# Moving six chunks of a modulation matrix product from TensorE to VectorE

## The chip, the cores and the metric

The kernel runs on one core of a Trainium2 chip. The metric is the device time of one execution in microseconds (us), as the median of three runs; lower is better. The engines are named as in the profile: PE is TensorE (matmul), PEld its weight loads, DVE VectorE, ACT ScalarE, POOL GpSimd, SP SyncE. Here SP issues the DMA loads of the weights.

## The reference

Two transformer blocks over 256 tokens of 1024 features, all in float32. The first has an attention and pooling mixer and a mixture of 32 experts. The second is modulated by a vector that comes from a condition `c`:

```python
def second_block(x, c, w_ada, b_ada, norm1_g, norm2_g, w_in, ...):
    mod = jax.nn.silu(c) @ w_ada[l] + b_ada[l]          # (1, 1024) @ (1024, 6144)
    sh1, sc1, g1, sh2, sc2, g2 = jnp.split(mod[:, None, :], 6, axis=-1)
    hn = (_rms(x, norm1_g[l]) * (1 + sc1) + sh1).astype(x.dtype)
    y = _mixer(hn, w_in[l], ...)
    x = x + g1 * (y.astype(x.dtype) @ w_out[l])
    hn = (_rms(x, norm2_g[l]) * (1 + sc2) + sh2).astype(x.dtype)
    gate, up = jnp.split(hn @ w_gate_up[l], 2, axis=-1)
    x = x + g2 * ((jax.nn.silu(gate) * up) @ w_down[l])
    return x
```

The change concerns the first line, `mod`. It doesn't depend on `x`, so it can be computed whenever the weights are there.

## The kernel before

The program has these stages, in the times of the trace: the first block's mixer and the router (here called the head, 0 to about 108 us); its experts, for which 2 MB loads of weights stream in (to about 1029 us); the second block's mixer (to about 1199 us): the modulated input is transposed into columns, projected part by part (`fv`, `mo`, `fq`, `fk`, `mqk`, ... in the order of the table `PROJ`), and goes through three kinds of heads; then its feed-forward part, to the end.

Weights are loaded into a ring of slots. SP issues the loads in one order, each as soon as slots are free (`pump`); the program gives slots back with `release`. A weight that is used as a split in two float32r halves goes through `split`: ACT writes the high half (L311, or with a gain L318), DVE the low half (L312, or L319).

`mod` is made from 24 chunks of 1 MB of `w_ada`, called `("ada", i)`, 128 rows by 2048 columns (the last eight 2 x 128 rows by 1024). `GRPS` cuts them in runs: chunks 0 to 7 (needed for the mixer's input, computed in the head), 8 to 15 (the gate `g1`, computed in the mixer), 16 to 19 and 20 to 23. A run ends in 512 x 4 sums that ACT copies out (L881). `MODE` has a letter for each chunk:

- `p`: PE multiplies. Four matmuls (L873), one for each quarter of 512 columns, with 32 copies of a column of `cs` (silu of `c`) as the weights, sit on four column groups of the array and add into one PSUM tile. Below, these four are called a group.
- `d`: DVE multiplies the chunk's four quarters by `cs` in place. The first of a run does only that (L853); each later one adds the chunk before (L855), whose slots are then released. The last sum goes through PE as one more group, with ones instead of `cs`.

The first `p` of a run stands behind its `d`s, so the sum by ones comes in the group after. `ada_step` and `ada_to` are called at set places of the program (`ASTEP`, `QSTEP` and `STEPS` in the head, `ADAT` in the mixer). A scheduler then places each engine's instructions; those under `keep_in_program_order` keep their order among themselves. In the head, chunk 3 to 7 come between the attention pairs; beside them stand the attention's scaling of its result `ya` (L679), its transposition (L687), the pooled half's `bt` (L817) and the splits `wl` (L319) of the first block's output projection `w_op`. In the mixer, `modulate` computes for each pair of 128 features `ht` (DVE), the high half of `cols` (ACT) and the low half (DVE); `gates` is a chain of small DVE operations from `z` to `gl`; `heads` computes for `fq` and `fk` squares on ACT (L1439), their sums (L1440), a reciprocal root in short steps (L354 to L363) and the scaling (L1443) on DVE, and PE then transposes the result (L1451).

Of the kernel before, what the change touches and what calls it, by code (L numbers as in the profile page):

```python
# [156 lines left out]
W_R = ((0, 2), (2, 2), (4, 4))  # L157
WARM = (14, 24)
BD_AT = (9, 6)
MODE = "ddddpppp" "pppppppp" "ddpp" "pppp"  # L160
GRPS = (0, 8, 16, 20, 24)
STEPS = (3, 2, 0, 0)
ASTEP = 2
# [11 lines left out]
class Net:  # L175
# [655 lines left out]
    def ada_setup(self):  # L831
        nc, c = self.nc, self.const
        self.cs = c.tile([P, KD], F32, name="cs")
        v = self.vcol("c_2", 0, KD)
        nc.scalar.activation(self.cs, v, AF.Exp, bias=0.0, scale=-1.0)
        nc.vector.tensor_scalar(self.cs, self.cs, 1.0, None, op0=OP.add)
        nc.vector.reciprocal(self.cs, self.cs)
        nc.vector.tensor_tensor(self.cs, self.cs, v, op=OP.mult)
        self.mod = c.tile([P, 48], F32, name="mod")
        self.adan, self.aacc = 0, None  # L840
        self.mr = c.tile([P, 512], F32, name="mr")

    def ada_step(self, n):
        nc = self.nc
        for i in range(self.adan, self.adan + n):
            o, m, k, nk = ADA[i]
            first, last = i in GRPS, i + 1 in GRPS
            w = self.chunk(("ada", i)).rearrange("p a (b c) -> p (a b) c", c=512)
            if MODE[i] == "d":
                for j in range(4):  # L850
                    c = self.cs[:, k + j * nk // 4:k + j * nk // 4 + 1]
                    if first:
                        ins = nc.vector.tensor_scalar(w[:, j], w[:, j], c, None, op0=OP.mult)  # L853
                    else:
                        ins = nc.vector.scalar_tensor_tensor(w[:, j], w[:, j], c, self.aacc[1][:, j], op0=OP.mult, op1=OP.add)  # L855
                    self.tc.keep_in_program_order(ins)
                if not first:
                    self.release(self.aacc[0])
                self.aacc = ("ada", i), w
                if not last:  # L860
                    continue
            pieces = []
            if MODE[i] == "p":
                pieces.append((("ada", i), w, [self.cs[:, k + j * nk // 4:k + j * nk // 4 + 1] for j in range(4)]))
            if self.aacc and (last or MODE[i] == "p"):
                pieces.append((*self.aacc, [self.ones[:, 0:1]] * 4))
                self.aacc = None
            if first or MODE[i - 1] == "d":
                self.adap = self.tr()
                self.adas = True  # L870
            for x, (key, w, cs) in enumerate(pieces):
                for j in range(4):
                    ins = nc.tensor.matmul(self.adap[32 * j:32 * j + 32, :], lhsT=cs[j].to_broadcast([P, 32]), rhs=w[:, j],  # L873
                                           start=self.adas, stop=last and x == len(pieces) - 1, skip_group_check=True,
                                           tile_position=(0, 32 * j))
                    if j == 0:
                        self.tc.keep_in_program_order(ins)
                self.adas = False
                self.release(key)
            if last:  # L880
                nc.scalar.copy(self.mr, self.adap)  # L881
        self.adan += n

    def ada_to(self, n):
# [1013 lines left out]
```

## Time and profile before

| | |
|---|---|
| median of three runs | 1392.44 us (1392.4 to 1392.58) |
| profiled execution | 1393.41 us, span 1391.7 us |
| granted clock of PE, mean | 0.986 of full speed |
| PE busy | 1298.2 us, 93% of the span |
| DVE busy | 557.3 us, 40% |
| ACT busy | 313.3 us, 23% |
| weight traffic | 494.04 MB, 355 GB/s on the mean |

The span is the time between the first and the last instruction of the one profiled execution; 1.7 us lie around it. Busy shares are means over stages that have different limits; the stretches below tell them apart.

### The profile page before, as it was taken

To read this page: it belongs to the slowest core of one execution; us is meant where nothing else is said; L and a number is where in the kernel's file an instruction comes from. 1 tells how busy PE (TensorE), PEld (TensorE's weight loads), DVE (VectorE), ACT (ScalarE), POOL (GpSimd) and SP (SyncE) were. 2 spreads that over 40 slices of the span, in tenths; PEclk is the share of its full clock that TensorE was granted. 3 is DMA by queue.
4 is the path that set the end of the run, shared out by engine and by line. 5 is a ranking of instruction groups with operands and counts; after the bars stand their busy time and mean duration, and the time that the engine had idled before them with its cause. 6 is when DMAs were issued, how large, how long until landed. Compare 5 with 4: busy or idle time off the path is not lost. (4 is left out here: it accounts for less than half of the span.)

```text
span 1391.7 us, 17149 instructions
## 1 busy us (share of the span) xinstructions
PE 1298.2 (93%) x6988; PEld 705.6 (51%) x6988; DVE 557.3 (40%) x1163; ACT 313.3 (23%) x602; POOL 49.0 (4%) x161
## 2 busy tenths in 40 slices
PE   9999999999999989889879998989789999999998
PEld 8674333333333333233323333333238887799997
DVE  6753322222323222132311222222247877655555
ACT  5650000000000000000000000000045556544443
POOL 7200000000000000000000000000000000000000
PEclk9999999999999999999989999999999999999999
DMA  9689999999999999999999999999988464555520
GB/s 386 244 336 428 426 427 427 428 427 425 417 428 427 427 427 428 427 428 426 428 424 426 427 427 427 428 428 428 410 356 320 165 256 153 222 189 188 189 93 31
DMA packets 42470, 494.04 MB, mean 355 GB/s; under 512 B 4720, under 2 KB 4976, under 8 KB 8720
## 3 DMA queue, kind: packets, MB, share of 16 engines
q1 hardware_dynamic: 42240, 492.78, 85.2%
q8 instruction: 57, 0.93, 0.3%
q14 instruction: 29, 0.24, 0.0%
q10 hardware_dynamic: 144, 0.10, 0.0%
HBM read 491.81 MB, written 1.05 MB: 354 GB/s over the span
## 5 line engine op out<-in xcount | busy, mean ns | idle before, releaser
L1102 PE MATMUL acc<-ring,xg 128*64 128x512 f32 x1264 | 290.8, 608 | 12.9 <-DMA ring<-in_moe_dram 12.9
L1102 PE MATMUL acc<-extra,xg 128*64 128x512 f32 x784 | 176.8, 596 | 9.5 <-DMA extra<-in_moe_dram 9.5
L1102 PEld LDWEIGHTS acc<-ring,xg 128*64 128x64 f32 x1264 | 88.1, 139 | 191.6 <-issue 161.7
L312 DVE TENSOR_TENSOR ring<-ring,ring 128x1024 fp32r<-128x1024 f32 (+4 forms) x108 | 121.1, 1130 | 87.1 <-ACT ring L311 82.1
L1130 PE MATMUL tr<-ring,aT 128*64 128x512 f32 x640 | 144.7, 596 | 9.4 <-DMA ring<-in_moe_dram 8.6
L297 PEld LDWEIGHTS tr<-cols,ring 128*128 128x128 f32 x1056 | 128.0, 192 | 1.7 <-ACT cols L1349 0.8
L297 PE MATMUL tr<-cols,ring 128*128 128x256 f32 x1056 | 128.9, 283 | 0.0
L311 ACT CAST ring<-ring 128x1024 fp32r<-128x1024 f32 (+4 forms) x108 | 104.1, 974 | 103.9 <-PE tr L297 65.3
L1241 DVE TENSOR_SCALAR gc<-acc 128x512 f32<-128x512 f32 x32 | 22.1, 692 | 259.1 <-PE acc L1102 243.4
L1161 DVE SCALAR_TENSOR_TENSOR x<-tr,G,x 128x512 f32<-128x512 f32 x128 | 87.8, 744 | 74.6 <-PE tr L1157 74.6
L1102 PEld LDWEIGHTS acc<-extra,xg 128*64 128x64 f32 x784 | 53.5, 137 | 116.8 <-issue 97.5
L1137 DVE TENSOR_TENSOR uc<-tr,gc 128x512 fp32r<-128x512 f32 x32 | 22.1, 692 | 213.3 <-ACT gc L1136 213.3
L1242 ACT ACTIVATE sg<-gc 128x512 f32<-128x512 f32 x32 | 20.2, 632 | 342.8 <-DVE gc L1241 342.8
L1130 PEld LDWEIGHTS tr<-ring,aT 128*64 128x64 f32 x640 | 44.9, 137 | 92.0 <-issue 76.7
L1130 PE MATMUL tr<-extra,aT 128*64 128x512 f32 x384 | 86.6, 596 | 0.1
L1136 ACT CAST gc<-tr 128x512 fp32r<-128x512 f32 x32 | 18.8, 586 | 242.4 <-PE tr L1130 242.4
L297 PE MATMUL acc<-ring,cols 128*128 128x384 f32 (+3 forms) x384 | 69.3, 330 | 1.1 <-ACT cols L1349 0.5
L1119 ACT ACTIVATE aT<-tr 128x512 f32<-128x512 f32 x32 | 19.1, 598 | 214.0 <-PE tr L1117 214.0
L297 PEld LDWEIGHTS acc<-ring,cols 128*128 128x128 f32 x384 | 61.3, 188 | 9.0 <-issue 5.7
L1057 DVE SCALAR_TENSOR_TENSOR xg<-tr,vt,rg 128x256 f32<-128x256 f32 x60 | 26.2, 479 | 92.7 <-PE acc L1102 88.4
L297 PE MATMUL acc<-ring,q 128*128 128x512 f32 x176 | 56.7, 394 | 0.0
L1130 PEld LDWEIGHTS tr<-extra,aT 128*64 128x64 f32 x384 | 26.9, 137 | 48.4 <-issue 46.9
(429 smaller groups left out, 1314.6 us busy)
## 6 DMA issues: line engine op xcount, KB each, us to landing
ring<-in_moe_dram SPq DMA_DIRECT2D x117, 2048.0 KB, 37.2
extra<-in_moe_dram SPq DMA_DIRECT2D x73, 2048.0 KB, 38.5
ring<-in_rest_dram SPq DMA_DIRECT2D x69, 1024.0 KB, 6.9
ring<-in_rest_dram SPq DMA_DIRECT2D x11, 768.0 KB, 5.3
ring<-in_moe_dram SPq DMA_DIRECT2D x4, 1024.0 KB, 13.0
ring<-in_rest_dram SPq DMA_DIRECT2D x2, 780.0 KB, 12.0
ring<-in_rest_dram SPq DMA_DIRECT2D x3, 512.0 KB, 9.9
ring<-in_rest_dram SPq DMA_DIRECT2D x2, 528.0 KB, 7.1
```

The lines of the kernel that those rows point to most:

```text
L297: self.nc.tensor.matmul(out, lhsT=l, rhs=r, start=start, stop=stop, skip_group_check=True)
L311: i = nc.scalar.copy(hi, w)
L312: j = nc.vector.tensor_tensor(lo, w, hi, op=OP.subtract)
L1057: nc.vector.scalar_tensor_tensor(x[:, j, :], p[:, j * 256:(j + 1) * 256], self.vcol("g_ffn_norm", k + j), rg, op0=OP.mult, op1=OP.mult)
L1102: nc.tensor.matmul(d[64 * s:64 * s + 64, :], lhsT=xg[g, k - k % 2][:, k % 2, i * CAP:(i + 1) * CAP], rhs=w[:, o + s * 512:o + (s + 1) * 51 ...
L1119: nc.scalar.activation(aT.rearrange("p a b -> p (a b)"), p, AF.Copy, scale=0.5)
L1130: nc.tensor.matmul(pd[64 * s:64 * s + 64, :], lhsT=aT[:, k % 4, (k // 4) * 64:(k // 4) * 64 + 64], rhs=w[:, k % n, s * 512:(s + 1) * 512], ...
L1136: i = nc.scalar.copy(yh, pd)
L1137: j = nc.vector.tensor_tensor(yl, pd, yh, op=OP.subtract)
L1161: ins = nc.vector.scalar_tensor_tensor(d, p, self.G[:, tt, e:e + 1], d, op0=OP.mult, op1=OP.add)
L1241: nc.vector.tensor_scalar(gc, pg, 7.0, None, op0=OP.min)
L1242: nc.scalar.activation(sg, gc, AF.Tanh, scale=0.851)
```

## The change

Chunks 4 and 5 of the first run and 10 to 13 of the second change from `p` to `d`. As the `d`s of the second run no longer stand at its start, the code asks for the running sum (`self.aacc`) rather than for the run's start, and keeps the PSUM tile (`self.adap`) over the `d`s in between.

```diff
-MODE = "ddddpppp" "pppppppp" "ddpp" "pppp"
+MODE = "ddddddpp" "ppddddpp" "ddpp" "pppp"
...
-        self.adan, self.aacc = 0, None
+        self.adan, self.aacc, self.adap = 0, None, None
...
-                    if first:
+                    if not self.aacc:
                         ins = nc.vector.tensor_scalar(w[:, j], w[:, j], c, None, op0=OP.mult)
                     else:
                         ins = nc.vector.scalar_tensor_tensor(w[:, j], w[:, j], c, self.aacc[1][:, j], op0=OP.mult, op1=OP.add)
                     self.tc.keep_in_program_order(ins)
-                if not first:
+                if self.aacc:
                     self.release(self.aacc[0])
...
-            if first or MODE[i - 1] == "d":
+            if self.adap is None:
                 self.adap = self.tr()
                 self.adas = True
...
             if last:
                 nc.scalar.copy(self.mr, self.adap)
+                self.adap = None
```

In numbers: in the head, L873 has three groups instead of five, and DVE eight more L855. In the mixer (chunks 8 to 15), five groups instead of eight (8, 9, 14, the sum by ones, 15), and on DVE four more L853 and twelve more L855. Lines behind L858 have numbers higher by one in the changed kernel.

Where the scheduler puts them. First DVE in the head, around the scaling `ya` of one attention pair. Before:

```order
L532 RECIPROCAL sm_680<-sm_680 128x4
L855 SCALAR_TENSOR_TENSOR ring_61<-ring_61,cs,ring_65 128x512 x4
L679 TENSOR_TENSOR ya_756<-tr_709,sm_680 128x256
L532 RECIPROCAL sm_760<-sm_760 128x4
L319 SCALAR_TENSOR_TENSOR wl_902<-ring_64,vt,wh_901 128x512 x2
L319 SCALAR_TENSOR_TENSOR wl_920<-ring_64,vt,wh_919 128x512 x2
L689 TENSOR_TENSOR ring_66<-tr_779,ring_66 128x256
```

and now:

```order
L532 RECIPROCAL sm_680<-sm_680 128x4
L855 SCALAR_TENSOR_TENSOR ring_61<-ring_61,cs,ring_65 128x512 x4
L855 SCALAR_TENSOR_TENSOR ring_61<-ring_61,cs 128x512 x4
L855 SCALAR_TENSOR_TENSOR ring_62<-ring_62,cs,ring_61 128x512 x4
L679 TENSOR_TENSOR ya_751<-tr_709,sm_680 128x256
L532 RECIPROCAL sm_755<-sm_755 128x4
L817 TENSOR_SCALAR bt_799<-acc_798,psc_296,pbc_298 128x256
L524 ISA s_845,m_846<-acc_849,mask 128x128
L524 ISA m_846 128x1
```

The eight new L855 stand directly behind the four that were there, ahead of `ya`; the splits `wl` that followed `ya` stand further behind. On PE at that place the groups L873 (two chunks and the ones) stood before the transposition of `ya` (tr_779). Before:

```order
L297 MATMUL tr_733<-mg_300,t_74_536 128x128 x2
L297 MATMUL tr_733<-mg_300,t_74_536 128x16
L873 MATMUL tr_742<-ring_61,cs 32x512 x4
L873 MATMUL tr_742<-ring_61,ones 32x512 x4
L873 MATMUL tr_742<-ring_62,cs 32x512 x4
L687 MATMUL tr_779<-ident,ya_756 128x128 x2
L541 MATMUL tr_786<-ident,s_758 128x128 x3
L541 MATMUL tr_791<-ident,s_758 128x128 x3
L297 MATMUL acc_803<-t_118_717,ring_86 128x256
```

and now:

```order
L297 MATMUL tr_733<-mg_300,t_74_536 128x128 x2
L297 MATMUL tr_733<-mg_300,t_74_536 128x16
L297 MATMUL acc_798<-t_118_717,ring_86 128x256
L297 MATMUL acc_808<-t_118_717,ring_86 128x256
L297 MATMUL acc_849<-cols_552,cols_551 128x128
L297 MATMUL acc_849<-cols_552,cols_551 128x256
L297 MATMUL acc_857<-cols_552,cols_551 128x128
L297 MATMUL acc_857<-cols_552,cols_551 128x256
L687 MATMUL tr_774<-ident,ya_751 128x128 x2
```

The three groups are gone from here (three now stand further behind); a projection of the pooled half and scores come instead.

Second, DVE in the mixer where the input is modulated. Before:

```order
L1348 SCALAR_TENSOR_TENSOR ht_18180<-acc_18124,A_1379,rw_18169 128x256 x2
L1348 SCALAR_TENSOR_TENSOR ht_18188<-acc_18129,A_1379,rw_18169 128x256
L1350 SCALAR_TENSOR_TENSOR cols_18179<-ht_18180,mod,cols_18178 128x256 x2
L1368 TENSOR_TENSOR ring_18083<-ring_63,ring_18083 128x780
L1350 SCALAR_TENSOR_TENSOR cols_18179<-ht_18188,mod,cols_18178 128x256
L1348 SCALAR_TENSOR_TENSOR ht_18188<-acc_18129,A_1379,rw_18169 128x256
L1348 SCALAR_TENSOR_TENSOR ht_18195<-acc_18134,A_1379,rw_18169 128x256 x2
L312 TENSOR_TENSOR ring_18083<-ring_62,ring_18083 128x780
L1350 SCALAR_TENSOR_TENSOR cols_18179<-ht_18188,mod,cols_18178 128x256
```

and now, with `ring_65` the slot of chunk 10:

```order
L1349 SCALAR_TENSOR_TENSOR ht_18179<-acc_18124,A_1379,rw_18169 128x256 x2
L853 TENSOR_SCALAR ring_65<-ring_65,cs 128x512 x4
L1351 SCALAR_TENSOR_TENSOR cols_18178<-ht_18179,mod,cols_18177 128x256 x2
L1369 TENSOR_TENSOR ring_18083<-ring_63,ring_18083 128x780
L1349 SCALAR_TENSOR_TENSOR ht_18187<-acc_18129,A_1379,rw_18169 128x256 x2
L1349 SCALAR_TENSOR_TENSOR ht_18194<-acc_18134,A_1379,rw_18169 128x256
L1351 SCALAR_TENSOR_TENSOR cols_18178<-ht_18187,mod,cols_18177 128x256 x2
L1351 SCALAR_TENSOR_TENSOR cols_18178<-ht_18194,mod,cols_18177 128x256
L1349 SCALAR_TENSOR_TENSOR ht_18194<-acc_18134,A_1379,rw_18169 128x256
```

The four L853 stand between the first `ht` and the first `cols`, and the split (L312) that stood among the columns has moved behind them.

Third, where `fq` and `fk` are scaled, DVE. Before, from the first `fq` scaling on:

```order
L1443 TENSOR_TENSOR sq_18479<-acc_18399,rsh_18483 128x384
L1443 TENSOR_TENSOR sq_18479<-acc_18400,rsh_18483 128x384
L312 TENSOR_TENSOR ring_18083<-ring_62,ring_18083 128x1024 x2
L1440 TENSOR_REDUCE ms_18559<-sq_18560 128x12
L354 TENSOR_SCALAR ms_18559<-ms_18559 128x12
L355 TENSOR_SCALAR rth_18565<-ms_18559 128x12
L356 TENSOR_SCALAR rsh_18564<-rth_18565 128x12
L361 TENSOR_TENSOR rth_18565<-rsh_18564 128x12
```

and now:

```order
L361 TENSOR_TENSOR rth_18488<-rsh_18487 128x12
L362 TENSOR_TENSOR rth_18488<-rth_18488,ms_18482 128x12
L363 SCALAR_TENSOR_TENSOR rsh_18487<-rth_18488,rsh_18487 128x12
L1441 TENSOR_REDUCE ms_18563<-sq_18564 128x12
L361 TENSOR_TENSOR rth_18488<-rsh_18487 128x12
L354 TENSOR_SCALAR ms_18563<-ms_18563 128x12
L362 TENSOR_TENSOR rth_18488<-rth_18488,ms_18482 128x12
L355 TENSOR_SCALAR rth_18569<-ms_18563 128x12
L363 SCALAR_TENSOR_TENSOR rsh_18487<-rth_18488,rsh_18487 128x12
L356 TENSOR_SCALAR rsh_18568<-rth_18569 128x12
L1444 TENSOR_TENSOR sq_18483<-acc_18403,rsh_18487 128x384
L1444 TENSOR_TENSOR sq_18483<-acc_18404,rsh_18487 128x384
```

`sq_18564` are the squares of `fk`, `sq_18483` those of `fq` (before: `sq_18560` and `sq_18479`). The sum for `fk` (L1440, now L1441) stood behind the scaling of `fq` and now stands ahead of it, in the middle of `fq`'s steps. PE transposes the scaled `fq` behind the last matmuls of `fk` and ahead of `mqk` (acc_18594) in the changed kernel:

```order
L297 MATMUL acc_18504<-ring_18122,cols_18177 128x384
L297 MATMUL acc_18504<-ring_18122,cols_18178 128x384
L297 MATMUL acc_18504<-ring_18122,cols_18177 128x384
L1452 MATMUL tr_18584<-ident,sq_18483 128x128 x3
L297 MATMUL acc_18594<-cols_18177,ring_18083 128x256
L297 MATMUL acc_18594<-cols_18178,ring_18083 128x256
L1452 MATMUL tr_18589<-ident,sq_18483 128x128 x3
```

and in the one before as well:

```order
L297 MATMUL acc_18500<-ring_18122,cols_18178 128x384
L297 MATMUL acc_18500<-ring_18122,cols_18179 128x384
L297 MATMUL acc_18500<-ring_18122,cols_18178 128x384
L1451 MATMUL tr_18580<-ident,sq_18479 128x128 x3
L1451 MATMUL tr_18585<-ident,sq_18479 128x128 x3
L297 MATMUL acc_18590<-cols_18178,ring_18083 128x256
L297 MATMUL acc_18590<-cols_18179,ring_18083 128x256
```

Only the work on DVE that feeds this transposition has moved.

## Rows read from the trace of the kernel before

**Rows 1.** The page: busy time, share and instructions of each engine.

```profile
PE 1298.2 (93%) x6988; PEld 705.6 (51%) x6988; DVE 557.3 (40%) x1163; ACT 313.3 (23%) x602; POOL 49.0 (4%) x161
```

**Rows 2.** Busy time of the engines by stretches, granted clock, DMA share, GB/s.

```profile
55.00:80.00 25.00, 24.80 (x170) 18.44 (x169) 17.10 (x52) 19.07 (x58) 0.00 (x0) 1.00 0.52 194
66.00:72.00 6.00, 6.00 (x48) 4.63 (x48) 2.98 (x9) 4.63 (x13) 0.00 (x0) 1.00 0.00 0
90.00:100.00 10.00, 9.89 (x58) 7.82 (x56) 4.68 (x8) 4.61 (x12) 0.53 (x2) 1.00 1.00 408
100.00:1000.00 900.00, 827.87 (x4019) 317.18 (x4020) 241.74 (x417) 65.00 (x115) 10.09 (x30) 0.98 1.01 426
1040.00:1100.00 60.00, 59.08 (x399) 51.03 (x399) 45.86 (x132) 33.64 (x62) 0.00 (x0) 1.00 0.68 260
```

**Rows 3.** Waits of the DMA queue (SP), 50 to 100 us: total, times, longest.

```profile
SPq L248 <- DVE wl L319: 16.6, 2, 11.6
```

**Rows 4.** SP's issues around 90 us: start, duration.

```profile
90.14 0.33 SPq L248 DMA_DIRECT2D ring<-in_moe_dram  x1
```

**Rows 5.** DVE in order of time, head: start, duration, line, [idle before].

```profile
51.66 2.71 DVE L855 SCALAR_TENSOR_TENSOR ring<-ring,cs,ring 128x512 f32<-128x512 f32 x4
54.28 0.42 DVE L679 TENSOR_TENSOR ya<-tr,sm 128x256 f32<-128x256 f32 x1
...
88.70 1.41 DVE L319 SCALAR_TENSOR_TENSOR wl<-ring,vt,wh 128x512 fp32r<-128x512 f32 x2 [0.50 <-ACT wh L318]
```

**Rows 6.** PE in order of time, head.

```profile
56.07 1.06 PE L873 MATMUL tr<-ring,cs 128*32 128x512 f32 x8
...
58.78 0.44 PE L687 MATMUL tr<-ident,ya 128*128 128x128 f32 x2
...
64.02 0.73 PE L297 MATMUL acc<-wh,ring 128*128 128x512 f32 x2 [0.20 <-ACT ring L819]
```

**Rows 7.** One line's instructions (L855, L853): ns min/median/max, first and last start.

```profile
L855 DVE SCALAR_TENSOR_TENSOR ring<-ring,cs,ring x12: 722/746/937, 34.9 to 1119.4; 128x512 f32<-128x512 f32 x12
...
L853 DVE TENSOR_SCALAR ring<-ring,cs x8: 474/482/708, 33.0 to 1105.7; 128x512 f32<-128x512 f32 x8
```

**Rows 8.** The chain of waits, 1030 to 1095 us: start, duration, what.

```profile
1041.46 0.49 DVE cols L1350
...
1042.00 7.71 PE acc L297 x41
1049.71 0.99 PE tr L873 x8
```

**Rows 9.** PE in order of time, mixer.

```profile
1038.08 1.06 PE L873 MATMUL tr<-ring,cs 128*32 128x512 f32 x8
...
1057.81 1.06 PE L873 MATMUL tr<-ring,cs 128*32 128x512 f32 x8
...
1078.37 0.82 PE L1451 MATMUL tr<-ident,sq 128*128 128x128 f32 x6
1078.94 5.99 PE L297 MATMUL acc<-cols,ring 128*128 128x256 f32 x48
```

**Rows 10.** DVE in order of time, mixer.

```profile
1054.16 0.71 DVE L312 TENSOR_TENSOR ring<-ring,ring 128x528 fp32r<-128x528 f32 x1 [3.01 <-ACT ring L311]
...
1067.75 0.18 DVE L1511 SCALAR_TENSOR_TENSOR gl<-z,gq 128x20 f32<-128x20 f32 x1
...
1075.28 1.02 DVE L1443 TENSOR_TENSOR sq<-acc,rsh 128x384 f32<-128x384 f32 x2
...
1079.09 0.95 DVE L1440 TENSOR_REDUCE ms<-sq 128x12 f32<-128x768 f32 x1 [0.46 <-ACT sq L1439]
```

**Rows 11.** One more stretch, as in rows 2.

```profile
38.00:44.00 6.00, 5.55 (x23) 3.63 (x23) 5.69 (x26) 2.88 (x6) 5.41 (x30) 0.72 0.76 315
```

**Rows 12.** PE in order of time, 34 to 50 us.

```profile
38.45 1.10 PE L297 MATMUL acc<-ring,t 128*128 128x512 f32 x2 [2.12 <-issue]
```

## The prediction

> **What bounds the kernel now.** I read the page first. TensorE (PE) is busy 93% of the span, VectorE (DVE) 40% [rows 1]; that alone would say that whatever is taken from PE is time won. The stretches say more [rows 2]. From 100 to 1000 us, the expert stage, the DMA share is 1.01 at 426 GB/s: the weights set the pace there, and what PE saves before or in it counts only if the stream of weights starts earlier. When it starts is in the view of the DMA queue's waits: the queue (SP) issues in order, each load waiting for its ring slots, and some of the longest waits of the head are for DVE's split of the output projection (wl, L319) [rows 3]. From the issue at 90.14 on [rows 4] the DMA share is 1.00 [rows 2]; the last of those splits starts at 88.70 and takes 1.41 us [rows 5]. From 1040 to 1100 us PE is busy 59.1 of 60 us and DVE 45.9 [rows 2]: there PE sets the pace, except where a short chain on DVE stands in front of it. So two places matter: how late the head's last splits are, and how far PE gets in the mixer of block 2.
>
> **The price of one chunk.** On PE a chunk is a group of four overlapping matmuls; three groups fill the time from 56.07 to 58.78 [rows 6], 0.9 us each, and one that stands alone holds the chain of waits for 0.99 us [rows 8]. On DVE it is four multiply-adds (L855) of 722 to 937 ns, or four multiplies (L853) of 474 to 482 ns at the median if it is the first of a run [rows 7]. The four of L855 at 51.66 delay the next start to 54.28 [rows 5]: 2.62 us. Four of L853 come to 4 x 0.48 = 1.9 us. So DVE pays two to three times what PE saves; what counts is whether it has the time where the new work lands.
>
> **Head.** Two chunks move (4 and 5). PE issues three groups where it had five (one by ones remains): 2 x 0.93 = 1.9 us less. DVE gets 2 x 2.62 = 5.24 us, all in one place: the order shows twelve L855 in a row ahead of ya (L679). So ya starts at 51.66 + 3 x 2.62 = 59.52 instead of 54.28 and ends 0.42 later. PE, without groups at 56.07, first does projections and scores that stood behind 58.78 (some 2.4 us), is at ya's transposition (L687) at 58.5 and waits to 60.0: 1.5 us. Transposes, a projection and the value matmuls then take it to about 62.2; it next wants the w_op matmul of the pooled half, for which two bt (L817) on DVE and a cast on ScalarE must come, now behind ya and a row of scores. I walk them to 61.5, 63.0 and 64.2. PE starts that matmul at about 64.3; before it was at 64.02 [rows 6]. Nearly equal, but before two groups were still to come and now three: +0.28 + 0.95, about **+1.2 us** at the splits that free the last slots, and the expert stage passes it on whole. The two loads whose slots the moved chunks themselves free come later too, but the DMA engines moved nothing from 66 to 72 us [rows 2], so these are hidden; if that gap were not there, they would cost their 1.5 us as well. Bounds: -1.9, if only PE's saving counts; +5.2, if all of DVE's work is exposed, which its idle time of 7.9 of the 25 us from 55 to 80 [rows 2] speaks against.
>
> **Mixer, modulation.** Before, chunk 10 ran on PE at 1038.08 [rows 9] in a gap in which PE waited for the modulated columns, so taking it away saves nothing. Now its four multiplies stand on DVE between the first ht (L1349; L1348 before) and the first cols (L1351; L1350): +1.9 us in the chain of waits that releases PE at 1042.00 [rows 8]. DVE's splits fall behind the cols, so PE's projection fv, which ended at 1049.7, ends at about 1052.1 by my walk, with four matmuls of the next one (mo, 0.13 each) done: +2.5 - 0.5 = **+2.0 us**.
>
> **Mixer, mo and the gate chain.** PE saves chunks 11 and 12 here, 2 x 0.99 [rows 8]. DVE gets eight multiply-adds, 5.24 us, in front of the last split for mo; the gap there is 3.01 us [rows 10]. They can start once the second z is there, about 1053.5, and end at 1058.8; with the split (0.71) it is 1059.5. PE has mo matmuls until about 1057.5, then waits 2.1 us, and mo ends at 1060.65 where it ended at 1057.81 [rows 9]. The gate chain behind it, on DVE alone, ended at 1067.93 with gl [rows 10] and now at about 1070.3: **+2.4 us so far**, with PE's saving in it.
>
> **Mixer, the heads.** Chunk 13 stands right behind gl, 2.6 us. The order costs more. Before, DVE scaled fq (L1443) at 1075.28 [rows 10], well before PE transposed it (L1451) at 1078.37, and with that PE went straight on to the 5.99 us of mqk [rows 9]. Now DVE's second sum of squares (L1441, for fk) stands ahead of the first L1444, and it waits for the end of fk on PE. PE in turn has the transposes of fq (L1452) right behind fk and ahead of mqk: each waits for the other's next step. From the end of fk, about 1079.9 now, it takes 0.7 to the sum's start (1079.09 against 1078.37 before [rows 9, 10]), 0.95 for the sum, some 0.7 for six short steps of two interleaved chains, and 0.5 for one scaling: 2.85 us until 1082.8, against 1078.37. **+4.4 us in all for the mixer**; what follows is the same work for PE. Bounds: -3.0 (three groups of 0.99 saved, all of DVE's 9.8 us in its 14.1 us of idle time from 1040 to 1100 [rows 2]); +7 (the three waits 2.0 + 2.1 + 2.85 with no saving against them).
>
> **The clock.** After PE's idle 2.12 us up to 38.45 the granted clock was 0.72 on the mean from 38 to 44 [rows 11, 12], a mixture of its levels 2.4 and 1.2 GHz; 0.28 x 6 = 1.7 us of PE were lost, say 1.5. Shorter waits may leave it alone; which of them do, this row can't tell. The change makes waits of about 1.5, 2 (modulation), 2.1 and 2.85 us. I take one such drop: **+1.5 us**, between 0 and 4 x 1.5 = 6. The Trainium skill, "TensorE: Matmul & The Clock Gate", part 1, says that an idle PE falls back to half its clock and gets the rest only by being busy again; it speaks against any change that opens gaps on a full PE, and the trace agrees with the 0.72 behind 2.12 us. Taken for all four waits, that would make the last term 6 and not 1.5.
>
> **Slots.** A chunk on DVE keeps its ring slot until the next one has read it, and 10 to 13 hold theirs some 10 us longer, so loads behind them start later. By the waits I get fq1 landed at 1058.7 (wanted at 1060.5) and mqk1 at 1084.6 (wanted from 1085). That is hidden, barely: cost 0; if one is late, 1 to 4 us.
>
> **Sum.** 1.2 + 4.4 + 1.5 = +7.1 us on the profiled execution's 1393.4: 1400.5. The runs' median is 1.0 lower (1392.44): **1399.5 us**.
>
> **Rivals.** *PE's saving is what counts* (faster). The new work lands in DVE's idle time, and PE is shorter by 1.9 us in the head and 3.0 in the mixer. For it: rows 2. Against it: three places where the new work stands ahead of what PE wants next. It holds if DVE is through at each of them before PE gets there: 1392.4 - 4.9 = 1387.5; half of it, 1390. Chance 0.12. The Trainium skill, "Perfetto Trace Analysis", identifying the most-contended engine, would relieve the most occupied engine first, PE here by busy time, though it warns that matmul busy time is a poor measure.
>
> *It cancels.* The third group of the head hides in a wait (0 to +0.3), no clock drop, fk's wait half as long: +0 to +2.5, 1392 to 1395. Chance 0.2.
>
> *The forecast*, 1396 to 1403: chance 0.5.
>
> *Loads or clock on top*: mqk1 or fq1 late, or the clock falls in three or four places: 1403 to 1408. Chance 0.18.
>
> **Numbers.** The runs shown lie within 0.2 us; 0.2%, 2.8 us, is about what can be told from no change, so faster is below 1389.7 and slower above 1395.2: 0.1, 0.2 and 0.7. The range leaves out half of the first rival and the end of the last: 1390 to 1405.
>
> **What would show it.** ya (L679) at 59.5; PE idle 1.5 us before L687 and 2 us before the first w_op matmul; the issue that was at 90.14 at about 91.4, and all of the expert stage as much later; the first cols 1.9 us later against ht; a wait of PE for the last mo split, and one of 2 to 3 us for sq (L1444) before L1452; a granted clock under 1.00 between 1040 and 1100. I am wrong if the issue comes before 90, if PE doesn't wait for sq, or if DVE is through with the eight multiply-adds before PE wants the split.

## The result and the profile after

The changed kernel takes 1407.32 us (median of six runs, 1406.58 to 1408.58); the kernel before took 1392.51 us on the same chip. The ratio is 1.0097 (95% interval 1.0086 to 1.0109): 13.5 us slower, or 12.0 to 15.2 (14.8 by the two medians). The direction was forecast, the size was not: 1399.5 us was the number and 1405 the end of the range. The profiled execution took 1408.58 us, span 1406.9, against 1391.7.

Busy times on the page of the changed kernel, for [rows 1]:

```profile
PE 1303.6 (93%) x6948; PEld 712.1 (51%) x6948; DVE 571.3 (41%) x1187; ACT 313.0 (22%) x602; POOL 49.2 (3%) x161
```

PE has 40 records fewer, the five groups of eight, and is busy 5.4 us longer: what is left takes longer. The stretches show where (columns as in [rows 2]: busy time of PE, PEld, DVE, ACT and POOL, then granted clock, DMA share and GB/s):

```profile
35.00:46.00 11.00, 8.93 (x36) 5.34 (x35) 10.31 (x34) 5.13 (x9) 9.28 (x42) 0.84 0.69 285
55.00:65.00 10.00, 8.26 (x50) 7.54 (x49) 7.70 (x20) 8.18 (x21) 0.00 (x0) 0.83 0.41 138
66.00:72.00 6.00, 5.57 (x29) 4.46 (x30) 5.32 (x14) 3.81 (x12) 0.00 (x0) 1.00 0.12 51
1040.00:1100.00 60.00, 52.05 (x285) 44.55 (x278) 45.37 (x115) 26.28 (x41) 0.00 (x0) 0.88 0.65 250
1042.00:1055.00 13.00, 10.41 (x43) 9.50 (x44) 11.30 (x24) 5.93 (x12) 0.00 (x0) 0.74 0.57 178
1062.00:1072.00 10.00, 7.96 (x40) 7.63 (x40) 7.55 (x16) 4.60 (x8) 0.00 (x0) 0.83 1.00 413
1088.00:1100.00 12.00, 9.17 (x63) 8.85 (x62) 9.02 (x27) 4.12 (x6) 0.00 (x0) 0.86 0.82 340
```

From 1040 to 1100 us the clock was 1.00 before [rows 2] and is 0.88 now. One minus the clock, times the length, is the time at full speed that PE lost: 3.4 us from 1042 to 1055, 1.7 from 1062 to 1072, 1.7 from 1088 to 1100, 6.8 us in the mixer, and 1.7 from 55 to 65 in the head. The first stretch (35 to 46) is the fall that was there before [rows 11]. In slices of 1 us the clock is 0.50 (1.2 GHz) from 1044 to 1050 us; from 1051 to 1062 it is 1.00 (2.4 GHz). These figures are PE's work lost; how much later the kernel ends by them is worked out below.

PE's waits from 1028 to 1100 us (total, times, longest):

```profile
PE tr L1452 <- DVE sq L1444: 2.8, 1, 2.8
PE acc L297 <- DVE ring L312: 2.0, 1, 2.0
...
PE acc L297 <- ACT cols L1350: 1.5, 1, 1.5
PE acc L297 <- DVE cols L1351: 1.4, 1, 1.4
```

PE in order of time (start, duration, [idle before]), at the places of [rows 6] and [rows 9]:

```profile
60.54 0.54 PE L687 MATMUL tr<-ident,ya 128*128 128x128 f32 x2 [1.74 <-DVE sm L532]
...
64.79 0.71 PE L297 MATMUL acc<-wh,ring 128*128 128x512 f32 x2
...
1043.05 0.45 PE L297 MATMUL acc<-ring,cols 128*128 128x390 f32 x1 [1.53 <-ACT cols L1350]
1044.88 2.00 PE L297 MATMUL acc<-ring,cols 128*128 128x390 f32 x5 [1.38 <-DVE cols L1351]
1047.04 15.29 PE L297 MATMUL acc<-ring,cols 128*128 128x390 f32 x86 [0.16 <-DVE ht L1349]
1064.37 1.91 PE L297 MATMUL acc<-ring,cols 128*128 128x264 f32 x7 [2.04 <-DVE ring L312]
...
1078.00 1.05 PE L873 MATMUL tr<-ring,ones 128*32 128x512 f32 x4
...
1079.70 1.04 PE L873 MATMUL tr<-ring,ones 128*32 128x512 f32 x2
...
1081.40 1.04 PE L873 MATMUL tr<-ring,ones 128*32 128x512 f32 x2
...
1091.80 0.90 PE L1452 MATMUL tr<-ident,sq 128*128 128x128 f32 x3 [2.83 <-DVE sq L1444]
```

Three of the waits that were forecast are there at nearly their size: 1.74 us before L687 (1.5 forecast), 2.04 for the mo split (2.1), 2.83 for sq (2.85). The modulation's wait (2 forecast) is there as two, 1.53 and 1.38 us, where the kernel before has 0.54, 0.19 and 0.34. The first of those three:

```profile
1039.69 0.45 PE L297 MATMUL acc<-ring,cols 128*128 128x390 f32 x1 [0.54 <-ACT cols L1349]
```

One is missing: PE was to idle 2 us before the first w_op matmul, and its row at 64.79 has no idle time. Something that was not forecast is there as well. A group has eight records, two for each of its four matmuls, and takes 1.06 us where it stands together [rows 9]. The mixer's sum by ones now goes out in three lots, two matmuls, one and one, with matmuls of a projection (128x384) between them, and each lot takes 1.04 to 1.05 us.

DVE in order of time, for [rows 5] and [rows 10]:

```profile
57.32 2.73 DVE L855 SCALAR_TENSOR_TENSOR ring<-ring,cs,ring 128x512 f32<-128x512 f32 x4
59.97 0.42 DVE L679 TENSOR_TENSOR ya<-tr,sm 128x256 f32<-128x256 f32 x1
...
91.72 1.41 DVE L319 SCALAR_TENSOR_TENSOR wl<-ring,vt,wh 128x512 fp32r<-128x512 f32 x2 [0.96 <-ACT wh L318]
...
1042.77 1.66 DVE L853 TENSOR_SCALAR ring<-ring,cs 128x512 f32<-128x512 f32 x4
1044.35 0.87 DVE L1351 SCALAR_TENSOR_TENSOR cols<-ht,mod,cols 128x256 fp32r<-128x256 f32 x2
...
1058.31 5.38 DVE L855 SCALAR_TENSOR_TENSOR ring<-ring,cs,ring 128x512 f32<-128x512 f32 x8
1063.61 2.44 DVE L312 TENSOR_TENSOR ring<-ring,ring 128x528 fp32r<-128x528 f32 x3
...
1076.37 0.18 DVE L1512 SCALAR_TENSOR_TENSOR gl<-z,gq 128x20 f32<-128x20 f32 x1
1076.47 2.73 DVE L855 SCALAR_TENSOR_TENSOR ring<-ring,cs,ring 128x512 f32<-128x512 f32 x4
...
1089.71 0.95 DVE L1441 TENSOR_REDUCE ms<-sq 128x12 f32<-128x768 f32 x1
...
1091.19 1.02 DVE L1444 TENSOR_TENSOR sq<-acc,rsh 128x384 f32<-128x384 f32 x2
```

DVE's prices are as costed: four L855 delay the next start by 2.65 us, eight by 5.30, four L853 by 1.58. SP's issue of [rows 4], the start of the expert stage's stream:

```profile
93.17 0.33 SPq L248 DMA_DIRECT2D ring<-in_moe_dram  x1
```

It comes 3.0 us later than at 90.14. With these rows the 15.2 us between the two spans fall to four places: 3.0 in the head; 5.6 from there to gl (L1512 at 1076.37, before at 1067.75 [rows 10]: 8.6 less 3.0); 4.8 from gl to the first transposition of sq (1091.80, before at 1078.37 [rows 9]: 13.4 less 8.6); and 1.8 behind that, from the last fall on. Forecast were 1.2, 2.4, 2.0 and one fall of 1.5 somewhere.

### The profile page after: what moved, and what is told of

It is laid out like the page before. It is cut to its first block, busy times and chain, and to the rows that moved or that the text cites. A ratio compares the mean times of both kernels' runs of the same rounds, so it can differ in the third digit from the quotient of the medians.

```text
span 1406.9 us, 17091 instructions
## 1 busy us (share of the span) xinstructions
PE 1303.6 (93%) x6948; PEld 712.1 (51%) x6948; DVE 571.3 (41%) x1187; ACT 313.0 (22%) x602; POOL 49.2 (3%) x161
## 3 DMA queue, kind: packets, MB, share of 16 engines
HBM read 491.81 MB, written 1.05 MB: 350 GB/s over the span
## 5 line engine op out<-in xcount | busy, mean ns | idle before, releaser
L1103 PE MATMUL acc<-ring,xg 128*64 128x512 f32 x1264 | 285.9, 599 | 13.1 <-DMA ring<-in_moe_dram 13.1
L1103 PE MATMUL acc<-extra,xg 128*64 128x512 f32 x784 | 179.7, 604 | 10.0 <-DMA extra<-in_moe_dram 10.0
L312 DVE TENSOR_TENSOR ring<-ring,ring 128x1024 fp32r<-128x1024 f32 (+4 forms) x108 | 121.0, 1130 | 89.5 <-ACT ring L311 87.9
L297 PE MATMUL acc<-ring,cols 128*128 128x384 f32 (+3 forms) x384 | 73.6, 344 | 5.1 <-DVE ring L312 2.0
L297 PEld LDWEIGHTS acc<-ring,cols 128*128 128x128 f32 x384 | 64.8, 199 | 12.9 <-issue 6.4
## 6 DMA issues: line engine op xcount, KB each, us to landing
ring<-in_rest_dram SPq DMA_DIRECT2D x3, 512.0 KB, 13.2
```

The source lines that it names most:

```text
L297: self.nc.tensor.matmul(out, lhsT=l, rhs=r, start=start, stop=stop, skip_group_check=True)
L312: j = nc.vector.tensor_tensor(lo, w, hi, op=OP.subtract)
L1103: nc.tensor.matmul(d[64 * s:64 * s + 64, :], lhsT=xg[g, k - k % 2][:, k % 2, i * CAP:(i + 1) * CAP], rhs=w[:, o + s * 512:o + (s + 1) * 51 ...
```

## The experiments

Ratios are to the kernel before, measured beside each kernel on the same chip; times are medians. All but the last two are edits of the changed kernel.

**The two halves.** Only the head's chunks (`"ddddddpp" "pppppppp"`), and only the mixer's (`"ddddpppp" "ppddddpp"`).

```diff
-MODE = "ddddddpp" "ppddddpp" "ddpp" "pppp"
+MODE = "ddddddpp" "pppppppp" "ddpp" "pppp"
```

> Only chunks 4 and 5 move; the mixer is as before. Theory (waits of PE behind DVE's new work, and half a clock after each such wait): the first issue of the expert stage that was at 90.14 comes 3.0 us later, 1.3 of it from PE's waits and 1.7 from the clock, and 2.7 of it reach the end: 1395.2 us. Waits alone, without the clock: 1393.8. PE's saved groups are what counts: 1390.6.

> Only chunks 10 to 13 move; the head is as before. Theory: the rest of the 14.8 us, about +12, 1404.6 us, with the same three waits of PE in the mixer (columns, last split of mo, sq before its transposition) and three falls of the granted clock. If head and mixer acted on each other the two runs would not add up to +14.8.

Head: 1397.06 us (six runs from 1394.1 to 1399.8; 1395.2 expected), 1.0025 (1.0011 to 1.0038), +3.5. Mixer: 1409.03 us (1404.6 expected), 1.0108 (1.0092 to 1.0125), +15. Most of the loss is the mixer's. The halves do not add up: the mixer alone is as slow as the whole change. Its profile has a further fall, at a place where neither the kernel before nor the changed kernel shows one (both 1.00 there):

```profile
1175.00:1230.00 55.00, 52.39 (x330) 39.61 (x330) 36.67 (x89) 31.76 (x66) 0.00 (x0) 0.94 0.47 178
```

0.06 x 55 = 3.3 us. Without it the mixer would stand at about +12, which is the changed kernel less its head. Why the clock falls there in this kernel is open.

**One chunk back to PE.** From the mixer alone, chunk 13 (`"ppdddppp"`) or chunk 10 (`"pppdddpp"`) returns.

```diff
-MODE = "ddddddpp" "ppddddpp" "ddpp" "pppp"
+MODE = "ddddpppp" "ppdddppp" "ddpp" "pppp"
```

> Mixer only, with chunk 13 back on PE. In the order of DVE the scaling of fq then stands ahead of fk's sum again. Theory: the wait for sq goes (2.8 us) and the clock stays up after it (1.5 us), one group on PE comes back (0.9): 1404.6 - 3.4 = about 1401. Rival: the wait for sq comes from fk being late and not from the order: then it stays, and the time is 1404 or more.

> Mixer only, with chunk 10 back on PE, where its group ran in a gap; 11 to 13 stay on DVE. Theory: the first columns come 1.7 us earlier, the two waits of 1.5 and 1.4 us ahead of fv fall back to 0.5 and 0.5, one multiply-add turns into a multiply at the start of the run (0.8 us less on DVE ahead of mo's last split), and the clock has one reason less to fall: 4 to 5 us faster than the mixer-only run, 1.0075 of the kernel before. Rival: the columns were hidden by the splits behind them, 0 to 1 faster, 1.0105.

Without chunk 13: 1400.9 us, 1.0056 (1.0039 to 1.0073), near the 1401 expected, though that was reckoned from the 1404.6 which the mixer alone did not keep to; the wait for sq is gone and the clock is 1.00 from 1085 to 1100. Without chunk 10: 1400.24 us, 1.0047 (1.0031 to 1.0064), where 1.0075 was expected; the mixer's first fall is gone (1.00 from 1040 to 1050) with the first wait for cols at 0.54 us as before, while the clock still falls between 1072 and 1100 (0.89 to 1088, 0.86 from there). Against the mixer alone these are 7 and 8.5 us less, of which 3.3 are that kernel's further fall, which neither of them shows. The rest is 4 and 5 us. It is not the price of a wait and its fall alone: without chunk 13 the sum by ones, too, goes out in one piece, which the section on the broken sum prices by itself:

```profile
1065.10 1.80 PE L873 MATMUL tr<-ring,ones 128*32 128x512 f32 x8
```

**The clock by itself.** Unread matmuls, on data that is there before the wait ends and into a PSUM tile that nobody reads, fill the waits of the changed kernel in four places.

```diff
+                    if i == 0:
+                        self.warm(14)
...
+            self.warm(24)
...
+                    if name == "mo" and h and q:
+                        u = self.tr()
+                        for i in range(16):
+                            self.mm(u[:, :n], Xh[:, 0, 0:P], s[0][:, 0, :], True, True)
...
+                if out is qT0:
+                    self.warm(22)
```

> The whole change, with PE kept busy by matmuls whose results nothing reads, in the places where it waited: 14 ahead of the head's transposition of ya, 24 ahead of the modulated columns, 16 ahead of the last split of mo, 22 ahead of the transposition of sq. The order of everything else is that of the changed kernel. Theory: the waits stay, but the clock stays at 1.00 behind them, and that is worth 1.7 + 2 + 1.5 + 1.5 = 6.7 us less what the extra matmuls delay, at most 1: about 1401. Rival (the waits alone make the loss, the clock only falls where PE has to wait for DVE anyway): 1407 to 1409.

> The changed kernel once more, as the measure for the runs beside it on the same chip: 1407.3 us where the kernel before takes 1392.5, so 1.0107 of whatever that takes here; less if the chip or the clock's falls differ.

> The changed kernel, as the measure for the next run on the same chip: 1.010 of the kernel before.

> The kernel with filled waits of run e4 again, now beside the changed kernel on one chip. Theory (half a clock behind the waits is a good part of the loss): 4 to 6 us faster than e9. Rival: within 1 us of it, and the difference seen before was one of chips.

Filled: 1403.25 us, 1.0073 (1.0056 to 1.009), against 1407.47, 1.0094 (1.0077 to 1.0111), of the changed kernel on another chip (4.2 us by the medians, 2.9 by the ratios). Beside each other on one chip: 1402.11 us, 1.0059 (1.0042 to 1.0075), against 1406.94, 1.0098 (1.0081 to 1.0115), so 4.8 us. In the traces PE's order is that of the changed kernel with the 76 extra matmuls put in. DVE has the same work, PE has more, and the kernel ends sooner: that is the share of the falls. (The profile of the last one still shows a fall of 1.7 us from 1042 to 1055, the first one's none.)

**The broken sum.** The sum by ones is issued with its four matmuls kept in order, last one first.

```diff
-                for j in range(4):
+                for j in (3, 2, 1, 0) if cs[0] is cs[3] else range(4):
...
-                    if j == 0:
+                    if j == 0 or cs[0] is cs[3]:
```

> The whole change, but the four matmuls of a sum by ones are kept together (the last quarter first). In the changed kernel's trace those for chunks 10 to 13 stand in three pieces at 1078.0, 1079.7 and 1081.4, each as long (1.0 us) as a whole group. Theory: two pieces less, 2.0 us less on PE, all of it on the path, since the sum for fk waits for PE's end of fk: 2.0 us faster than the changed kernel. Rival: DVE's own steps set when sq comes, then 0 to 0.5.

> The whole change, but chunk 13 is taken two places later (the table ADAT), so that DVE's multiply-adds for it stand behind the scaling of fq and fk. Theory: as in the run with 10 to 12, the wait for sq (2.8 us) and the fall of the clock behind it (1.5) go: 4 to 4.5 us faster than the changed kernel, with the same number of chunks on DVE. Rival: the wait moves to the next user of DVE, the score part behind mqk: 0 to 2 faster.

In one piece: 1402.9 us, 1.0064 (1.0047 to 1.0081), 4.6 less than the changed kernel of that chip where 2.0 were expected. The other kernel asks for chunk 13 two steps later (`ADAT = (10, 11, 13, 13, 13, 15, ...` for `13, 15, 15, 15`). That takes the wait for sq from 2.8 to 0.6 us, but saves only 2.0 us, 1405.48, 1.0084 (1.0067 to 1.01). Its PE, in order of time:

```profile
1088.12 1.51 PE L873 MATMUL tr<-ring,ones 128*32 128x512 f32 x4
...
1090.12 1.04 PE L873 MATMUL tr<-ring,ones 128*32 128x512 f32 x2
...
1092.01 1.04 PE L873 MATMUL tr<-ring,ones 128*32 128x512 f32 x2
```

The sum is broken here too, now among the matmuls of mqk behind that wait: the transposition of sq comes 6.8 us sooner against the mixer's start (L1339) than in the changed kernel, and the way from it to the end takes 4.1 us longer.

**Both, on one chip.** The 4.6 us might have counted the clock's loss a second time, so the two edits were run singly and together.

> The changed kernel again, as the base of three others on the same chip. Both theories: 1406.5 to 1407.5 us.

> The changed kernel with the sum by ones of chunk 13 in one piece. The split alone is worth 2.1 us (two pieces more, 1.04 us each), so 1405 us; measured on another chip it was 4.6 us. If the clock also stays up behind the wait for sq, as in that profile, 1403 us again.

> The changed kernel with unread matmuls in its four waits of TensorE; the sum by ones stays in three pieces. 1402.2 us, as twice before (4.2 and 4.8 us less than the changed kernel).

> Both edits. Theory: two separate terms were missing from the sum, the falls of the clock (4.5 us) and the broken sum by ones (2.1 us or more); then both together give 1407 - 4.5 - 2.1 = 1400.4 us at most, 1398 us if the 4.6 us of the one edit are all its own: the 1399.5 us that were forecast without them. Rival: the gain of the one-piece sum was mostly the clock's, and both remove the same loss: 1402 us, as the filled kernel alone.

| | us | ratio (95%) | PE's work lost to the clock in the mixer, us |
|---|---|---|---|
| changed | 1407.86 | 1.0106 (1.0092 to 1.0121) | 6.5 |
| one piece | 1403.99 | 1.0076 (1.0062 to 1.009) | 5.1 |
| filled | 1401.68 | 1.0058 (1.0045 to 1.0071) | 0 |
| both | 1399.80 | 1.0045 (1.0032 to 1.0058) | 0 |

The last column is worked out as above from the same three stretches of one profile of each; for the kernel with both edits these are

```profile
1042.00:1055.00 13.00, 11.43 (x68) 10.54 (x66) 10.83 (x23) 6.63 (x14) 0.00 (x0) 1.00 0.56 195
1062.00:1072.00 10.00, 10.00 (x62) 8.91 (x62) 8.36 (x28) 4.71 (x9) 0.00 (x0) 1.00 0.78 325
1088.00:1100.00 12.00, 12.00 (x93) 10.84 (x92) 6.97 (x21) 6.25 (x15) 0.00 (x0) 1.00 0.70 286
```

and its PE, its SP and its DVE have

```profile
1076.07 1.06 PE L875 MATMUL tr<-ring,ones 128*32 128x512 f32 x8
...
1085.50 0.52 PE L1461 MATMUL tr<-ident,sq 128*128 128x128 f32 x3 [0.49 <-DVE sq L1451]
```

```profile
91.67 0.33 SPq L248 DMA_DIRECT2D ring<-in_moe_dram  x1
```

```profile
1072.33 0.18 DVE L1521 SCALAR_TENSOR_TENSOR gl<-z,gq 128x20 f32<-128x20 f32 x1
```

The same four profiles, cut at these places, say how much later than in the kernel before each stage ends, in us:

| | up to the issue | from there to gl | to the first transposition of sq | to the end |
|---|---|---|---|---|
| changed | 0.5 | 5.9 | 4.8 | 1.7 |
| one piece | 1.8 | 5.7 | 2.5 | 0.2 |
| filled | -0.2 | 1.9 | 4.9 | 0.3 |
| both | 1.5 | 3.1 | 2.6 | 0.3 |

Two prices can be read from it singly. From gl to the transposition of sq it takes 15.4 to 15.5 us in all eight profiles with chunks 10 to 13 on DVE at these places and the sum in three lots, waits filled or not, and 13.1 to 13.2 in the three with the sum in one piece: the two extra lots cost 2.3 us (two of 1.04 are 2.1). From that transposition to the end it takes 314.9 to 315.1 us in the four profiles of the changed kernel and 313.5 to 313.6 in the six of filled and one-piece kernels: the fall behind the wait for sq costs 1.5. With the lots that makes 3.8 of the 3.9 us of the one piece. It goes with either edit, so the two overlap (3.9 and 6.2 us by the medians, 8.1 together); why it goes with the one piece, where the wait stays, is open. The mixer's other falls stand between the issue and gl: 5.3 to 5.9 us in the changed kernel, 3.1 and 3.2 in two filled ones (4.3 in one that kept a fall, 1.9 in one where the fall ahead of the mixer, which the kernel before has too, is shorter). So they cost some 2.5 us, and the three together some 4.0 us of time for 6.5 of PE's work; that the rest would have been waited away is likely but not shown. The rival, one loss counted twice, has the last two rows of the first table equal; they differ by 1.9 us, but their intervals overlap, and it is the 2.3 us between gl and sq that speak against it. What is left of the change is 5.9 us, 0.45%.

**The kernel before.** It has falls of its own, around the mixer's start and in the head. One edit fills the first, the second also starts chunks of the head at other places.

```diff
+            self.warm(14)
             ps = self.columns(y)
...
-ASTEP = 2
-QSTEP = (0, 1)
+ASTEP = 1
+QSTEP = (0, 2)
```

> The kernel before, with 14 matmuls of which nothing is read ahead of the transposition at 1030.46, where PE had idled 1.54 us and the clock was 0.50 to 1036. Nothing else changes in the order. Theory: at full clock PE would be through with the transposes and chunks 8 and 9 some 2.2 us earlier, but the next matmul (L1325) needs rbz from DVE, which ends at 1036.15: 1.2 us faster than before, 1391.2. Rival: the clock is of no account where PE waits for others: no change.

> Neither the change nor more chunks on DVE: the kernel before with 14 unread matmuls ahead of 1030.46 as in e8, and with chunk 1 taken behind the rotary step of the queries (QSTEP, ASTEP), so that DVE's 2.9 us for it no longer stand ahead of what PE waits 2.12 us for at 38.45. Theory, the same as for the loss: that wait and the clock's fall behind it (1.5 us) go, the head ends 2 to 3 us earlier, with e8's 1.2: 0.9975 of the kernel before. Rival: a load that waits for the chunk's slot comes later and eats it: 0.9990, as e8.

With the fill alone: 1392.66 us against 1394.27, 0.9989 (0.9979 to 0.9999). The clock is 1.00 from 1028 to 1045, but PE now meets a wait of 0.6 us for rbz (L1325) that it did not have: some of the time returned is waited away. With the order changed too: 1392.57 us, 0.9999 (0.9989 to 1.0008), where 0.9975 was expected: no gain. In its head PE's wait has not gone but moved, 2.51 us ahead of 36.83 in place of 2.12 ahead of 38.45. No fall follows it, and the issue of [rows 4] comes 0.5 us sooner (89.66); it did so in the run before as well (89.77), with the old order and no fall there either. But the clock falls later:

```profile
1175.00:1230.00 55.00, 52.42 (x363) 44.05 (x362) 34.84 (x69) 30.32 (x57) 0.00 (x0) 0.97 0.48 189
```

0.03 x 55 = 1.7 us. No version made here beats the kernel before by more than about 0.1%.

## Why the prediction was wrong in size

**What bounds the kernel** held: the issue of the expert stage's stream and PE's way through the mixer decided, and the five groups less bought nothing, since PE waited.

**The price of a chunk** held: 2.65 us for four L855 against 2.62, 1.58 for four L853 against 1.9.

**Head, +1.2.** ya started at 59.97 (59.5 said) and PE waited 1.74 us (1.5). The walk behind that failed: the wait for bt is not there, and PE is at the w_op matmul at 64.79 (64.3 said) only because half a clock slowed it; in a second profile of the changed kernel, without a fall from 55 to 65, it is there at 63.53. The sum came out nevertheless, in part by luck. The issue is at 93.17, and in that second profile at

```profile
91.76 0.33 SPq L248 DMA_DIRECT2D ring<-in_moe_dram  x1
```

Part of the difference to 90.14 lies ahead of the new work. From the matmul L541 in front of it to the issue it takes 38.5 to 38.6 us in all six profiles with chunks 4 and 5 on PE, 39.6 to 39.7 in the nine with them on DVE and no fall in between, 41.1 and 41.2 where the clock falls from 55 to 65:

```profile
51.59 0.44 PE L541 MATMUL tr<-ident,s 128*128 128x128 f32 x2 [0.16 <-ACT s L530]
...
51.98 0.44 PE L541 MATMUL tr<-ident,s 128*128 128x128 f32 x2 [0.16 <-ACT s L530]
```

(the first before, the second changed). So the step measured +1.0, and the fall 1.6 more where it came. The head alone measured +3.5; its profile has two falls of 1.7 us that the kernel before hasn't, one from 71 to 75 and one behind 1175, and lacks the one that [rows 11] show.

**Modulation and gate chain, +2.4.** Without falls: gl at 1072.33 with the issue at 91.67, so 4.6 - 1.5 = +3.1. In the changed kernel +5.6. The 2.5 on top are the clock's; the other 0.7 is what the walk missed.

**Heads, +2.0 beyond that.** The circle between fk's sum and fq's transposition was read rightly: 2.83 us. With both edits the transposition comes 7.1 us later than before, gl 4.6: +2.5. In the changed kernel +4.8, of which 2.3 are the broken sum.

**The clock, +1.5: the step that failed.** "I take one such drop", the text said, and put four at 6. In each of the four profiles of the changed kernel the clock falls behind the modulation's waits, the wait for the mo split and the wait for sq, and takes 6.5 to 6.8 us of PE's work in the mixer alone; in two of them it falls in the head too. In time that is 4.0 us in the mixer and 1.6 in the head, and the filled kernels got 4.8 and 6.2 us back. The modulation's two waits, 1.53 and 1.38 us, brought not one fall but a stretch of twice the length (3.4 us lost). The price of a fall was about right; that one wait in four would bring one had no row behind it. The Trainium skill, "TensorE: Matmul & The Clock Gate", part 1, says that an idle PE falls back to half its clock; taken for all four waits that was the 6, and the trace agrees with it (5.6 us of time where the head's fall is there) and not with the choice. That waits as short as these do it most of the time is what the runs show and not what the page says.

**A term that was missing: +2.3.** The prediction costed chunk 13 on DVE and left its sum by ones at the price of one group. The scheduler sends it out in three lots, and each lot costs what a whole group does.

**Slots, 0,** held. None of PE's new waits from 1028 to 1100 us is for a load, and in the head the DMA engines still have their gap from 66 to 72 us (share 0.12).

Sum without clock: 5.6 forecast. Without clock and lots the three places make 1.0 + 3.1 + 2.5 = 6.6; with both edits 5.9 were measured (7.4 by the profiled spans). With 4.0 for the mixer's falls and 2.3 for the lots it is 12.9, and 14.5 where the head's fall comes too; 12.0 to 15.2 were measured. Of the four cases the last, "Loads or clock on top", named the clock, with a chance of 0.18 and 1408 as its end; none named the lots.

## What to carry to other kernels

Where PE is full, a wait that an edit opens on it can cost more than its length: price the clock's fall for each of them (here 1.7 us of PE's work, or 3.4 where two waits followed closely), and take the fall as likely (14 of 16 in the four profiles of the changed kernel, with the modulation's two waits taken as one) but not as certain. Look in the order for how the moved work's leftovers are issued: a group that was one overlapped unit may come apart and pay in full for every piece. A wait that can't be closed can still be filled with matmuls that nobody reads. To price one step of a long kernel, measure between two marks close to it: the whole time mixes it with falls elsewhere.

## What the hardware showed that was not expected

The same wait does not always bring a fall. Behind the 2.83 us for sq the clock was 0.86 from 1088 to 1100 in the changed kernel. With the sum by ones in one piece the wait is 2.83 us again, up to 1088.33, and the clock stays at 1.00, in both profiles of that kernel; the wait and the stretch in the second:

```profile
1088.33 0.55 PE L1452 MATMUL tr<-ident,sq 128*128 128x128 f32 x3 [2.83 <-DVE sq L1444]
...
1088.00:1100.00 12.00, 11.68 (x89) 10.50 (x90) 7.79 (x26) 5.67 (x12) 0.00 (x0) 1.00 0.93 384
```

In the head, 1.74 us were followed by a fall from 55 to 65 in two of four profiles of the changed kernel. The row from which the forecast took its price is no different: the wait ahead of 39 us is in all 17 profiles with that order, and the clock from 35 to 46 is 0.84 in nine of them and 1.00 in eight, with 2.07 us of idle time in one of the nine and 2.10 in one of the eight. What decides it besides the length of a wait is open.

One matmul of L873 by itself takes 1.04 us, two together 1.05 (1.51 in the kernel with chunk 13 later) and four 1.06: what looks like a quarter of a group's work costs the whole.
